# Moving a 64-token tile from the dense expert path to the gathered one, in a one-core decoder-layer kernel

## The chip, the cores and the metric

The kernel runs on one core of a Trainium2 chip. The metric is the device time of one execution in microseconds; lower is better.

## The reference

One layer of a decoder trunk is computed for two groups of tokens with the same weights: a prompt of 1024 tokens and 8 samples of 8 tokens. The layer is RMSNorm, a combined input projection whose columns feed two mixers side by side (retention with 8 heads and RWKV-7 with 8 heads), an output projection, a residual, then a product-key expert mixer (PEER), a residual, a gated per-layer embedding and a last norm. The part around the change is PEER:

```python
q = (xb @ wq).reshape(PEER_BLOCK, PEER_HEADS, 2, PEER_DKEY // 2)
s = jnp.einsum('phcd,hcnd->phcn', q, keys).astype(jnp.float32)
sv, si = lax.top_k(s, PEER_TOPK)
cand = sv[:, :, 0, :, None] + sv[:, :, 1, None, :]
cv, ci = lax.top_k(cand.reshape(PEER_BLOCK, PEER_HEADS, PEER_TOPK * PEER_TOPK), PEER_TOPK)
...
gsm = jax.nn.softmax(cv, axis=-1)
hval = jnp.einsum('pd,phkd->phk', xb, u_tab[e])
act = (jax.nn.gelu(hval.astype(jnp.float32), approximate=False) * gsm).astype(xb.dtype)
return jnp.einsum('phk,phkd->pd', act, v_tab[e])
```

Each token chooses 16 experts in each of 8 heads, 128 of 16384, and each expert is a row of 1024 floats in `u_tab` and one in `v_tab`.

## The kernel before

The tokens are cut into nine tiles: tiles 0 to 7 are the prompt, 128 tokens each, and tile 8 holds the 64 sample tokens (`SIZE`, line 199). PEER is done in two ways.

*Gathered* (tiles 0 and 1, `E0`, and tiles 2 and 3, `G1`): `gather` (line 1115) fetches, for each of the 128 chosen experts, one row of `u_tab` for each of 128 tokens by an indirect DMA on GpSimd (line 1124), multiplies it with the token's row and sums on VectorE (line 1137), applies the gelu and the gate, then fetches the rows of `v_tab` and adds them up in an accumulator in PSUM (line 1151). A fetched tile is 128 x 1024 floats. The result goes to `yd` in memory.

*Dense* (tiles 8, 4, 5, 6, 7, `G2`, 576 tokens): all 16384 experts are computed for all tokens of the group. `hidden` (line 1246) makes the products with `u_tab` for 128 experts at a time, 128 times, each as three matmuls of split operands for 8 blocks of the model width (`mm3`, lines 328 to 330), and a gelu. `gates` (line 1221) builds from the chosen experts a dense gate matrix with one-hot tiles (lines 1235 to 1241) and stores it in `wd`. `act` (line 1262) multiplies the two and splits, and `dense` (line 1275) multiplies with `u`'s partner `v_tab` and adds up in `yT` (lines 1294 and 1301). Columns are cut by `chunks_of` (line 208) into equal parts of at most 512: 576 becomes 288 and 288, so that every weight tile is used in two matmuls.

The order of the work is this. `group_a` makes the input projections; `group_b` (line 650) runs the mixers of the tiles in the order of `BORDER`, as generators that are stepped in turn, with the output projection `c_rows` of finished tiles and, one step at a time, the generator `early` (line 1206). `early` makes the query and the top-k of tile 0 by `early_query` (line 1168), starts tile 0's gather, makes tile 1's query in between as soon as tile 1's rows are there, and then gathers tile 1. At most `EB` = 150 steps of it are taken in `group_b`; what is left is recorded at line 1483, after the query of the dense group (`c_query`, line 1008, in three parts: tiles 2 and 3; 8, 4 and 5; 6 and 7). Then a loop (line 1500) goes over the dense tiles: top-k of one beside the gates of the one before, then a share of the first 96 `hidden` products, stored in `gd`; the gathers of tiles 2 and 3 are recorded in its second and fifth turn (`TK1`). After it `dense_fused` (line 1304) makes the last 32 hidden products beside the first part of the output product, `dense_stored` (line 1323) reads the 96 stored ones back, and `ple` (line 1368) ends the layer tile by tile.

The order in which each engine finally takes its instructions is set by a list scheduler, which takes the recorded order as priority. Row buffers of the early gather are the four tags of `rows` (line 1208), and a fifth for the second tile. PSUM has eight banks: six in `psum` with two for the early accumulator (`psume`), later two for the accumulator `psumg` and six for the rest; in the dense stage `py` has two buffers of two banks.

## Time and profile before

| | |
|---|---|
| runs, us | 3994.43, 4011.38, 4012.78 (median 4011.38) |
| profiled execution, us | 3997.31 |
| its span, us | 3995.5 |
| instructions | 65022 |
| memory read and written, MB | 926.92 and 113.25 |
| mean over the span, GB/s | 260 |

The engine lines of the profile give busy time and its share of the span; the slices are fortieths of the span, some 100 us each. PE is TensorE's matmul, PEld its weight load, DVE VectorE, ACT ScalarE, POOL GpSimd and SP SyncE. In a row of groups the time after the bar is the sum of busy time and the mean of one instruction in ns; after the second bar stands the idle time just before them, with what ended it. Matmuls overlap in the pipeline, so their mean duration is longer than the distance from one to the next. In a row of a window the first number is its length and then comes the busy time of each engine with its count of instructions.

### The profile page before, as it was taken

The numbers are of one execution on the slowest core, as the hardware profiler recorded it, in microseconds if no ns is written. First come the engines' busy times: TensorE is split into PE (matmuls) and PEld (weight loads), VectorE is DVE, ScalarE is ACT, GpSimd is POOL, SyncE is SP. The second block draws the span as 40 slices with busy tenths as digits, with TensorE's granted clock in tenths as the row PEclk, the third lists the DMA queues.
The fourth block names the chain that finished last, engine by engine and source line by source line (L and its number), as shares of the span: only waits on it lengthen the run. The fifth ranks groups of instructions, "written<-read, shape, count | busy, mean of one in ns | idle before, by whom it ended". The sixth has DMA issues, their size and how long they took to land. (4 is left out here: it accounts for less than half of the span.)

```text
span 3995.5 us, 65022 instructions
## 1 busy us (share of the span) xinstructions
PE 3499.3 (88%) x24160; PEld 3210.9 (80%) x24160; DVE 3015.0 (75%) x5720; ACT 1242.6 (31%) x2374; POOL 2090.5 (52%) x1811
## 2 busy tenths in 40 slices
PE   8789986777867888579989999998999899899998
PEld 7688975545746666469989999998999888899977
DVE  4453588977798788761699999975999999995544
ACT  4232221111111121123354667782222222222222
POOL 5363175544456555451346778756767566561110
PEclk9799995567877787689999999999999999999999
DMA  7267467899868898994336889899998999995522
GB/s 259 73 198 239 158 225 256 265 309 285 302 222 295 304 320 285 349 320 146 130 123 220 321 304 352 307 348 333 326 320 316 345 339 360 336 369 183 164 80 70
DMA packets 458774, 1044.47 MB, mean 261 GB/s; under 512 B 71643, under 2 KB 194777, under 8 KB 451930
## 3 DMA queue, kind: packets, MB, share of 16 engines
q0 software_dynamic: 147456, 536.94, 37.9%
q1 hardware_dynamic: 248878, 390.11, 29.6%
q10 hardware_dynamic: 62124, 113.27, 7.5%
q8 instruction: 191, 3.13, 0.3%
q14 instruction: 125, 1.02, 0.1%
HBM read 926.92 MB, written 113.25 MB: 260 GB/s over the span
## 5 line engine op out<-in xcount | busy, mean ns | idle before, releaser
L1124 POOL DMA_INDIRECT grow<-in_pv,eid x512 | 526.3, 1028 | 506.7 <-DVE gacc L1151 386.8
L1151 DVE SCALAR_TENSOR_TENSOR gacc<-grow,ac,gacc 128x1024 f32<-128x1024 f32 x508 | 651.7, 1283 | 95.8 <-DMA grow<-in_pv,eid 90.6
L1124 POOL DMA_INDIRECT grow<-in_pu,eid x512 | 520.8, 1017 | 373.9 <-DVE grow L1137 246.1
L1137 DVE SCALAR_TENSOR_TENSOR grow<-grow,gacc 128x1024 f32<-128x1024 f32 x512 | 613.6, 1211 | 65.6 <-DMA grow<-in_pu,eid 64.6
L328 PE MATMUL ph<-cx,uh 128*128 128x288 f32 x2048 | 615.6, 301 | 29.3 <-ACT geh L1259 29.3
L330 PE MATMUL ph<-cx,ul 128*128 128x288 f32 x2048 | 615.2, 300 | 0.0
L329 PE MATMUL ph<-cx,uh 128*128 128x288 f32 x2048 | 615.1, 300 | 0.0
L1294 PE MATMUL py<-ah,vh 128*128 128x288 f32 x2048 | 442.3, 299 | 27.0 <-DVE yT L1301 15.6
L1294 PE MATMUL py<-ah,vl 128*128 128x288 f32 x2048 | 443.5, 299 | 23.3 <-POOL vl L303 13.5
L1294 PE MATMUL py<-al,vh 128*128 128x288 f32 x2048 | 443.5, 299 | 5.0 <-DVE al L301 4.8
L328 PEld LDWEIGHTS ph<-cx,uh 128*128 128x128 f32 x2048 | 389.3, 190 | 31.5 <-ACT geh L1259 31.5
L329 PEld LDWEIGHTS ph<-cx,uh 128*128 128x128 f32 x2048 | 389.5, 190 | 0.0
L330 PEld LDWEIGHTS ph<-cx,ul 128*128 128x128 f32 x2048 | 389.4, 190 | 0.0
L303 POOL TENSOR_TENSOR ul<-uraw,uh 128x1024 fp32r<-128x1024 f32 x128 | 307.1, 2400 | 150.7 <-ACT uh L299 132.4
L1294 PEld LDWEIGHTS py<-ah,vh 128*128 128x128 f32 x2048 | 330.1, 190 | 35.9 <-ACT vh L299 18.6
L1294 PEld LDWEIGHTS py<-ah,vl 128*128 128x128 f32 x2048 | 331.9, 191 | 29.6 <-POOL vl L303 15.9
L1294 PEld LDWEIGHTS py<-al,vh 128*128 128x128 f32 x2048 | 332.2, 191 | 7.2 <-DVE al L301 7.2
L303 POOL TENSOR_TENSOR vl<-vraw,vh 128x640 fp32r<-128x640 f32 (+2 forms) x112 | 166.9, 1490 | 224.6 <-ACT vh L299 223.5
L299 ACT ACTIVATE vh<-vraw 128x640 fp32r<-128x640 f32 (+2 forms) x224 | 151.9, 688 | 332.9 <-PE py L1294 292.0
L1301 DVE TENSOR_TENSOR yT<-yT,py 128x576 f32<-128x576 f32 x216 | 161.0, 747 | 95.6 <-PE py L1294 95.1
L1237 ACT ACTIVATE oh<-oh,it 128x128 f32<-128x128 f32 x576 | 182.4, 393 | 75.9 <-DVE oh L1235 74.9
L1235 DVE TENSOR_TENSOR oh<-csta,pit 128x512 f32<-128x512 f32 x288 | 184.0, 678 | 24.5 <-PE pwt L1240 24.3
(402 smaller groups left out, 7950.6 us busy)
## 6 DMA issues: line engine op xcount, KB each, us to landing
uraw<-in_puT SPq DMA_DIRECT2D x128, 512.0 KB, 4.4
vraw<-in_pvd SPq DMA_DIRECT2D x152, 320.0 KB, 4.9
wd<-wst ACTq DMA_DIRECT2D x36, 1024.0 KB, 14.2
wt<-wd SPq DMA_DIRECT2D x64, 576.0 KB, 7.1
cw<-in_w_out SPq DMA_DIRECT2D x128, 256.0 KB, 5.5
gd<-geh ACTq DMA_DIRECT2D x96, 288.0 KB, 5.0
ge<-gd SPq DMA_DIRECT2D x96, 288.0 KB, 5.5
wraw<-in_w_ret SPq DMA_DIRECT2D x48, 512.0 KB, 4.9
```

What stands on the lines that cost most here:

```text
L299: nc.scalar.activation(hi, src, AF.Copy)
L303: nc.gpsimd.tensor_tensor(lo, src, hi.bitcast(F32), op=OP.subtract)
L328: mm(out, lh(k), rh(k), start=first and k == 0, stop=False)
L329: mm(out, lh(k), rl(k), start=False, stop=False)
L330: mm(out, ll(k), rh(k), start=False, stop=last and k == nk - 1)
L1124: nc.gpsimd.indirect_dma_start(out=g[:n], out_offset=None, in_=src, in_offset=bass.IndirectOffsetOnAxis(ap=self.eid[t][:n, j:j + 1], axis=0))
L1137: nc.vector.scalar_tensor_tensor(g[:, c], g[:, c], 1.0, x[:, c], op0=OP.mult, op1=OP.mult, accum_out=hv[:, i, j:j + 1])
L1151: nc.vector.scalar_tensor_tensor(y[:, c], g[:, c], ac[:, j:j + 1], y[:, c], op0=OP.mult, op1=OP.add)
L1235: nc.vector.tensor_tensor(oh[j], io, p[:, j, s + b:s + b + 4, None].to_broadcast([128, 4, 128]), op=OP.is_equal)
L1237: nc.scalar.activation(oh[0][:, j], oh[0][:, j], AF.Copy, scale=it[:, s + b + j:s + b + j + 1])
L1294: nc.tensor.matmul(p[:, c, :cn], lh[:, b, :], rh[:, c0:c0 + cn], start=b == 0 and j == 0, stop=b == nb - 1 and j == 2)
L1301: nc.vector.tensor_tensor(yv, yv, pv, op=OP.add)
```

## The change

Tile 8 joins the gathered tiles: `E0` becomes `[0, 1, 8]` and `G2` `[4, 5, 6, 7]`, so that the dense group has 512 tokens, one chunk. A fetch of the gather has 128 rows, and tile 8 has 64 tokens; its 128 experts are therefore laid in two halves, the first 64 on partitions 0 to 63 and the others on 64 to 127, and 64 fetches of each table serve it. Its input row is loaded twice, its two partial sums go to `yd` as 128 rows, and `ple` adds both. Its query is the single-tile `early_query`, now for 64 rows, recorded behind tile 1's query with tile 0's gather in between, and ahead of the gathers of tiles 1 and 8. All gathers use one accumulator pool of two banks, opened at the start. `c_query` has two parts instead of three, the loop over the dense tiles one turn fewer, and `py` has four buffers of one bank.

```diff
-E0 = [0, 1]
+E0 = [0, 1, 8]
-G2 = [8, 4, 5, 6, 7]
+G2 = [4, 5, 6, 7]
...
-                    for _ in range(ERATE if self.rowed >= set(E0) else 0):
+                    for _ in range(ERATE if E0[1] in self.rowed else 0):
...
+        elif t == 8:
+            gsm = tp.tile([128, 128], F32, name="gsm8", tag="cf")
...
+        if t == 8:
+            ei = tp.tile([128, 128], I32, name="ei", tag="ex")
+            nc.vector.tensor_copy(ei[:n], ef[:n])
+            for k in range(2):
+                nc.scalar.dma_start(self.eid[t][64 * k:64 * k + 64], ei[:64, 64 * k:64 * k + 64])
+                nc.scalar.dma_start(self.gsm[t][64 * k:64 * k + 64], gsm[:64, 64 * k:64 * k + 64])
...
     def gather(self, gp, t, rows=("grow",), parts=1, acc=None):
-        n = 128
+        n = SIZE[t]
...
-        nc.sync.dma_start(x, self.xd[t])
+        for k in range(0, 128, n):
+            nc.sync.dma_start(x[k:k + n], self.xd[t][:n])
...
     def early(self, wp):
-        g = self.behind(self.gather(wp, E0[0], rows, acc=self.acc0), PG0)
-        while not self.rowed >= set(E0):
-            next(g, None)
-            yield
-        q = self.behind(self.early_query(wp, E0[1], "Wq", 1, ("Wq", "xT")), PQ1)
-        for _ in q:
-            next(g, None)
-            yield
+        g = self.gather(wp, E0[0], rows, acc=self.acc)
+        for t in E0[1:]:
+            while t not in self.rowed:
+                next(g, None)
+                yield
+            for _ in self.early_query(wp, t, "Wq", 1, ("Wq", "xT")):
+                next(g, None)
+                yield
         yield from g
-        yield from self.gather(wp, E0[1], rows + ("xT",), acc=self.acc0)
+        for t in E0[1:]:
+            yield from self.gather(wp, t, rows + ("xT",), acc=self.acc)
...
-                p = self.ps2.tile([128, 2, 512], F32, name="py")
+                p = self.ps2.tile([128, ncx, 512], F32, name="py")
...
-                y = tp.tile([128, D], F32, name="py", tag="njunk")
-                nc.sync.dma_start(y, self.yd[t])
-                nc.vector.tensor_tensor(h, h, y, op=OP.add)
+                for k in range(0, 128, n):
+                    y = tp.tile([128, D], F32, name="py", tag="njunk")
+                    nc.sync.dma_start(y[:n], self.yd[t][k:k + n])
+                    nc.vector.tensor_tensor(h[:n], h[:n], y[:n], op=OP.add)
...
+            acc = self.acc = self.pool("psumg", space=PS, es=eg, reuse_waits="tile")
             self.psums("psum", ep, a=2, b=3, d=1)
-            self.acc0 = self.pool("psume", space=PS, es=ep, reuse_waits="tile")
...
-            parts = [G1, G2[:QA], G2[QA:]]
+            parts = [G1, G2]
...
-            acc = self.pool("psumg", space=PS, es=eg, reuse_waits="tile")
...
-                    self.ps2 = self.pool("psumy", bufs=2, space=PS, es=e2, reuse_waits="tile")
+                    self.ps2 = self.pool("psumy", bufs=4 // len(self.chunks), space=PS, es=e2, reuse_waits="tile")
```

`early_query` takes `n = SIZE[t]` rows in place of 128 throughout.

More of the change, by code (lines that the diff above doesn't have):

```diff
@@ L181 @@
 CN = 2
-QA = 3
 BORDER = [1, 8, 2, 3, 4, 5, 6, 7]
@@ L187 @@
 IB = 2
-PG0 = 0
-PQ1 = 0
 PGT = "a"
@@ L1029, in c_query @@
                     nc.tensor.matmul(p[:SIZE[t], i * 128:i * 128 + 128], qT[:, off[t]:off[t] + SIZE[t]], kT, start=True, stop=True)
-                i0 = tiles.count(8)
-                if i0:
-                    nc.scalar.activation(s[:64, 0, hc % 2], p[:64, :128], AF.Copy)
-                nc.scalar.activation(s[:, i0:, hc % 2], p[:, i0 * 128:len(tiles) * 128].rearrange("p (t k) -> p t k", k=128), AF.Copy)
+                nc.scalar.activation(s[:, :, hc % 2], p[:, :len(tiles) * 128].rearrange("p (t k) -> p t k", k=128), AF.Copy)
                 if hc % 2:
@@ L1123, in fetch @@
             g = slot("grow", rows[j % len(rows)])
-            nc.gpsimd.indirect_dma_start(out=g[:n], out_offset=None, in_=src,
-                                         in_offset=bass.IndirectOffsetOnAxis(ap=self.eid[t][:n, j:j + 1], axis=0))
+            nc.gpsimd.indirect_dma_start(out=g, out_offset=None, in_=src,
+                                         in_offset=bass.IndirectOffsetOnAxis(ap=self.eid[t][:, j:j + 1], axis=0))
             return g
         x = slot("gx", rows[-1])
-        nc.sync.dma_start(x, self.xd[t])
+        for k in range(0, 128, n):
+            nc.sync.dma_start(x[k:k + n], self.xd[t][:n])
         xs, x = x, home()
         nc.scalar.activation(x, xs, AF.Copy)
-        hv = gp.tile([128, parts, 128], F32, name="hv")
+        hv = gp.tile([128, parts, 128], F32, name="hv")[:, :, :n]
         cs = [slice(i * D // parts, (i + 1) * D // parts) for i in range(parts)]
@@ L1138, in gather @@
             yield j
-        ac = gp.tile([128, 128], F32, name="ac")
+        ac = gp.tile([128, 128], F32, name="ac")[:, :n]
         for i in range(1, parts):
@@ L1189, in early_query @@
             for k in range(8):
[L1190 removed]
+                nc.tensor.matmul(p[:, :n], w[:, k], xT[:, k, :n], start=k == 0, stop=k == 7)
             qT = wp.tile([128, 128], F32, name="eqT", tag=("cf", "ef")[hc % 2])
[L1192 to L1194 removed]
+            nc.scalar.activation(qT[:, :n], p[:, :n], AF.Copy)
+            nc.tensor.matmul(p[:n, 128:256], qT[:, :n], kT, start=True, stop=True)
+            nc.scalar.activation(st[:n, hc % 2], p[:n, 128:256], AF.Copy)
             if hc % 2:
[L1196 removed]
+                nc.scalar.dma_start(self.sd[t][:n, hc - 1:hc + 1], st[:n])
             yield
@@ L1467, in build @@
             self.e12 = {}
-            n2, n3 = spans(G2[:QA])[1], spans(G2[:-1])[1]
-            query = self.c_query(cq, da, [(G1, x1), (G2[:QA], [y[:, :, :n2] for y in x]), (G2[QA:], [y[:, :, n2:] for y in x])])
+            n3 = spans(G2[:-1])[1]
+            query = self.c_query(cq, da, [(G1, x1), (G2, x)])
             def rest():
```

22 lines of the change are left out of this document (9 added, 13 removed).

## Prediction

> **What bounds the kernel now.** I read the page first: its engine totals and the 40 slices.
>
> ```profile
> span 3995.5 us, 65022 instructions
> PE 3499.3 (88%) x24160; PEld 3210.9 (80%) x24160; DVE 3015.0 (75%) x5720; ACT 1242.6 (31%) x2374; POOL 2090.5 (52%) x1811
> DVE  4453588977798788761699999975999999995544
> PEclk9799995567877787689999999999999999999999
> DMA  7267467899868898994336889899998999995522
> ```
>
> No engine binds everywhere, so I cut the span at landmarks of the program (first gather, the third tile's keys, first `wql`, first `oh`, first `yT`, the 64th, last gather, first `ppg`) and asked for busy time by stage. Columns: us, busy us of PE, PEld, DVE, ACT, POOL, granted clock, DMA share, GB/s.
>
> ```profile
> 1083.00:1725.00 642.00, 488.37 (x2648) 372.72 (x2647) 534.74 (x1013) 106.33 (x205) 352.83 (x350) 0.76 0.84 295
> 1725.00:2046.00 321.00, 299.09 (x2193) 288.44 (x2191) 183.34 (x736) 96.78 (x193) 124.95 (x94) 0.96 0.52 182
> 2046.00:2754.00 708.00, 666.26 (x5116) 661.08 (x5117) 627.29 (x1516) 466.06 (x989) 482.47 (x356) 0.98 0.81 296
> 2754.00:3163.00 409.00, 397.14 (x2958) 394.34 (x2957) 374.50 (x432) 110.90 (x188) 280.02 (x226) 0.99 0.92 326
> 3163.00:3600.00 437.00, 401.15 (x2860) 389.83 (x2860) 401.37 (x450) 117.30 (x173) 271.93 (x221) 0.97 0.98 349
> 3600.00:3835.00 235.00, 229.55 (x1716) 226.46 (x1714) 118.38 (x159) 63.32 (x94) 46.31 (x31) 1.00 0.50 156
> ```
>
> Mixers (to 1725): nothing saturated, a chain of waits with gathers in its gaps. Query and top-k (to 2046): PE 93%. Gates beside hidden products (to 2754): PE 94%, DVE 89%. Fused dense (to 3163): PE 97%, DMA 0.92. Stored dense with gathers (to 3600): DMA 0.98. Then 235 us of dense product alone, DMA at 0.50: room that no gather uses. Dense steps (`yT` additions) in these last three: 64, 95, 65.
>
> **The change, part by part.** *Price of the dense matmuls.* The chain has a run of 288-column ones, the order-of-time view 512-column ones in `ple` (first and last of 21 in a row):
>
> ```profile
> 3747.67 80.09 PE py L1294 x604
> ...
> 3928.08 0.39 PE L328 MATMUL ppg<-pga,pxh 128*128 128x512 f32 x1
> ...
> 3932.75 0.39 PE L330 MATMUL ppg<-pgx,pxl 128*128 128x512 f32 x1
> ```
>
> 80.09/604 = 0.1326 us each, and 4.67/20 = 0.2335. A pair of 288 (0.2652) becomes one of 512: 0.0317 us less. Hidden and output products are 3072 pairs each, so 6144 x 0.0317 = 195 us of PE time goes, and 16 x 24 x 0.0317 = 12 in the query, where 320 + 256 columns become 512.
>
> *Price of the gathers.* Tile 8 adds 64 + 64 fetches.
>
> ```profile
> L1124 POOL DMA_INDIRECT grow<-in_pv,eid x512 | 526.3, 1028 | 506.7 <-DVE gacc L1151 386.8
> L1151 DVE SCALAR_TENSOR_TENSOR gacc<-grow,ac,gacc 128x1024 f32<-128x1024 f32 x508 | 651.7, 1283 | 95.8 <-DMA grow<-in_pv,eid 90.6
> L1137 DVE SCALAR_TENSOR_TENSOR grow<-grow,gacc 128x1024 f32<-128x1024 f32 x512 | 613.6, 1211 | 65.6 <-DMA grow<-in_pu,eid 64.6
> L1137 DVE DVE_READ_ACCUMULATOR grow<-grow,gacc 128x1 f32 x512 | 40.8, 80 | 0.0
> q0 software_dynamic: 147456, 536.94, 37.9%
> ```
>
> One costs DVE (1283 + 1211 + 80)/2 = 1.287 us, POOL 1.03 us and the DMA 536.94/1024 = 0.524 MB. So +165 us DVE, +132 us POOL, +67 MB. Against that tile 8 leaves the gates, a ninth of the `oh`, `wst` and `wd` work below, and its top-k moves from the stage after the query into the mixers.
>
> ```profile
> L1235 DVE TENSOR_TENSOR oh<-csta,pit 128x512 f32<-128x512 f32 x288 | 184.0, 678 | 24.5 <-PE pwt L1240 24.3
> L1237 ACT ACTIVATE oh<-oh,it 128x128 f32<-128x128 f32 x576 | 182.4, 393 | 75.9 <-DVE oh L1235 74.9
> L303 POOL TENSOR_TENSOR ul<-uraw,uh 128x1024 fp32r<-128x1024 f32 x128 | 307.1, 2400 | 150.7 <-ACT uh L299 132.4
> L1241 ACT ACTIVATE wst<-pwt 128x512 f32<-128x512 f32 x144 | 157.6, 1106 | 43.6 <-PE pwt L1240 34.3 <-PE ph L330 4.6 <-issue 2.7
> L1050 DVE FIND_INDEX8 si<-sv,s 128x8 uint32<-128x128 f32 x96 | 25.9, 278 | 0.0
> L1088 DVE TENSOR_TENSOR eq<-csta,cf 128x800 f32<-128x800 f32 x64 | 80.1, 1251 | 0.3
> L1090 DVE TENSOR_REDUCE ef<-eq 128x16 f32<-128x800 f32 x64 | 62.4, 975 | 12.4 <-POOL eq L1089 12.3
> uraw<-in_puT SPq DMA_DIRECT2D x128, 512.0 KB, 4.4
> vraw<-in_pvd SPq DMA_DIRECT2D x152, 320.0 KB, 4.9
> wd<-wst ACTq DMA_DIRECT2D x36, 1024.0 KB, 14.2
> wt<-wd SPq DMA_DIRECT2D x64, 576.0 KB, 7.1
> gd<-geh ACTq DMA_DIRECT2D x96, 288.0 KB, 5.0
> ```
>
> A top-k costs DVE five passes like L1050 on 16 rows (80 x 0.27 = 22 us), eight `eq` and `ef` (8 x 142.5/64 = 18) and 40 short ones that I put at 5: 45 us, of 64 rows as of 128, since the row's length is the same. The `oh` of tile 8 are 32 x 0.678 = 22 us.
>
> *Where they go.* The lists of instructions of the two built programs give the order. When the query starts, 464 gather steps stand ahead on DVE before and 396 after; at the first `yT`, 703 and 804; at the 64th, 863 and 939; the last stands after the 159th of 224 `yT` before, after the 197th now. Before, PE has 17 of the 96 early hidden products ahead of the first gate matmul; after, 84. So the gates become a stage of their own, with DVE, ACT and DMA in it and little for PE.
>
> *Mixers.* The query of tile 8 stands between the third tile's and the fifth's chain, and tile 1's gather waits behind it in the program: two mixers with 19 and no gathers, then about as many as before; 68 fewer by the start of the query. Mixers and the fetches alone in them (us, POOL busy us and count, clock, DMA share, GB/s), and the matmuls of tile 1's query in the first of them:
>
> ```profile
> 957.00:1152.00 195.00, 66.34 (x67) 0.81 0.83 273
> 1152.00:1256.00 104.00, 36.59 (x35) 0.81 0.80 271
> 1256.00:1366.00 110.00, 47.98 (x49) 0.79 0.89 315
> L1190 PE MATMUL epq<-exT,ewq 128*128 128x128 f32 x191 | 32.8, 332 | 5.6 <-DMA ewq<-in_wq 4.7 <-ACT ktk L819 0.7
> ```
>
> 14 more fetches went with 6 us: 0.43 each, so 68 fewer are worth 29 us; were the mixers bound by fetches (110/49 = 2.2 each), 150. The new query has 256 such matmuls of half the width: at 32.8/191 each at most 44 us of PE, and if it stretches a mixer as tile 1's may have done (195 against 104), 91. I take 19 of the 44, since PE is idle a quarter of this stage: -29 + 19 = **-10** (ends -150 and +91; the mixers of 104 and 110 are the nearest rows). Its 16 weight loads of 512 KB go out on SP into one buffer, and its top-k on DVE, in a time without gathers: 45 us come, 68 x 1.287 = 88 go. Before 1083 the order is the same.
>
> *Query, top-k and hidden* (to the first `oh`). PE had 299 busy us, 17 hidden products (17 x 48 x 0.1326 = 108) in them; now 299 - 108 - 12 + 84 x 24 x 0.2335 = 650. DVE, in this stage and the gates together: 183 + 627 = 811 before, now 408 gather steps for 239 (+217), a top-k and its `oh` fewer (-67): 961, of which 385 fall to the gates (below) and 576 here. Fetches are 244 x 0.524 = 128 MB here, the rest as before. PE is the longest; at 96%: 677 us.
>
> *Gates.* 256 `oh` x 0.678 + 164 gathers x 1.287 = 385 us of DVE; ACT (182.4 + 157.6) x 8/9 = 302; PE 12 hidden products, 67 us, and the gate matmuls; DMA 164 x 0.524 = 86 MB of fetches, 32 x 1.05 = 34 of `wd`, some 16 of hidden and first dense loads. Rows for what such a mix reaches (all engines, then the fetches alone, then all engines again):
>
> ```profile
> 2300.00:2500.00 200.00, 192.20 (x1487) 191.33 (x1486) 193.13 (x487) 139.63 (x291) 155.78 (x118) 0.98 0.89 328
> 2500.00:2700.00 200.00, 63.55 (x66) 1.00 0.89 329
> 3300.00:3400.00 100.00, 91.57 (x643) 88.86 (x642) 95.91 (x98) 28.02 (x41) 65.10 (x54) 0.95 1.01 363
> ```
>
> 136 MB at 328 GB/s is 415 us, DVE's 385 at 92% are 418: I take 425. Both stages: 677 + 425 = 1102 against 321 + 708 = 1029, **+73**: PE's saving here is lost, since its work no longer lies beside the gates.
>
> *Fused dense.* 28 hidden products and 64 steps of 12: (672 + 768) x 0.2335 = 336 us of PE, at 97% 346; 135 gathers for 160, so DVE 375 - 25 x 1.287 and some 20 for narrower tiles = 323. Both would be over 90% busy: I take 352, against 409.
>
> *Stored dense, to the last gather.* 133 steps with 213 gathers, for 95 with 160. PE 133 x 15 x 0.2335 = 466. DVE: 401 - 160 x 1.287 = 195 for 95 steps, so 133 x 1.87 (eight ninths of most) + 213 x 1.287 = 523, at the 92% of before 570. DMA 112 MB of fetches, 44 of `vraw`, 44 of `ge` and `wt`, 5 of gate weights: 205 at 349 GB/s = 587. I take 577, against 437. The tail: 27 steps, the last eight of one block, 309 x 0.2335 = 72, against 235. Dense together 1001 against 1081: **-80**. PSUM: four one-bank `py` stand for two of two banks; PE waited 15.6 us for these at most, inside stages that DMA and DVE now set, so 0:
>
> ```profile
> L1294 PE MATMUL py<-ah,vh 128*128 128x288 f32 x2048 | 442.3, 299 | 27.0 <-DVE yT L1301 15.6
> ```
>
> The 205 MB are priced by the saturated rows (share 0.98 at 349 GB/s, 1.01 at 363). The Trainium skill, DMA: Bandwidth & Descriptors, "Where 436 GB/s comes from", puts the port ceiling at 435 GB/s and one core's share of the memory, both cores streaming, at about 358. By the first the estimate would be 471 us, DVE would bind at 570 and the sum would be 7 us less; the rows agree with the second, though one core runs here.
>
> *`ple`.* Tile 8 reads two halves of `yd` instead of eight transposes, in a stretch that PE fills: 0 (+-3). One accumulator pair for all tiles: gathers follow each other through it already; 0.
>
> Sum on the profiled run: 3997.3 - 10 + 73 - 80 = **3980**. Its runs had a median of 4011, 14 above it; 0.5% (20 us) is about what a measurement tells from no change.
>
> **Rivals.** (1) *The freed room is used.* For it: DMA stood at 0.52 from 1725 to 2046. If both stages before dense go at DVE's 961 us, 95% busy, they take 1012, -17, and if the query hides, the mixers give -29: 3997 - 29 - 17 - 80 = **3871**. Against it: PE alone wants 650 before the gates start, and DVE was 89% busy in the gates. (2) *The gate stage stalls.* From 2500 to 2700, with gates, 66 fetches took 200 us, 3.03 each; 164 at that price are 497 instead of 425: **4052**, slower. It decides from about 462 us for the stage. Against it: hidden loads shared the DMA there. (3) *The clock falls.* Stored dense leaves PE 80% busy, and mixers ran at 0.76 with PE 76% busy. At 0.76, 466 becomes 613: +36, **4016**; at half speed 932, far outside. Against it: 0.97 at 92%. The Trainium skill, TensorE: Matmul & The Clock Gate, "HAM oscillation", says that idle gaps over about 3.4 us drop the array to half clock. The longest wait of PE between 3130 and 3600 is 2.9 us (us in all, times, longest), so by that rule the clock stays:
>
> ```profile
> PEld py L1294 <- POOL vl L303: 12.5, 7, 2.9
> ```
>
> (4) *It doesn't do what it says*: the lists show that it does, no chance given.
>
> **How the numbers follow.** Forecast 3980, own range 3945 to 4015: 0.42, 0.19 of it faster by 0.5%, 0.02 slower (a mixer stretched by the query). Room used: 0.26. Gate stage stalls: 0.24. Clock: 0.08, half within 0.5%. Faster 0.19 + 0.26 = 0.45; slower 0.02 + 0.24 + 0.04 = 0.30; same 0.21 + 0.04 = 0.25. Range 3860 to 4075: from the first rival, with a little of the fetches' larger price, to the second with a quarter of the query's larger one.
>
> **What would show it.** `py` at 0.23 us a matmul, a tail near 72 us, first `oh` some 680 us after the first `wql` and the first `yT` some 425 later, PE well under 70% busy between. Wrong would be: mixers of 80 us where no gathers stand (then faster), gathers at over 3 us in the gates, or a clock under 0.9 in stored dense (slower).

## The result, and the profile after

The changed kernel takes 4112.38 us (median of 4 runs, 4101.5 to 4121.27) against 4011.59 for the kernel before in the same session: a ratio of 1.026, 95% interval 1.022 to 1.030. It is slower by about 100 us, and outside the range of the prediction. One of the four executions of the third experiment below took 9462.73 us, in a slow state, and is left out of its median. The page of the changed kernel, engine totals and slices:

```profile
span 4117.0 us, 52401 instructions
PE 3449.2 (84%) x17749; PEld 2831.4 (69%) x17749; DVE 3165.3 (77%) x5876; ACT 1172.9 (28%) x2149; POOL 2212.5 (54%) x1939
DVE  4453579877881588776799988898799989999844
PEclk9799986577775678769999999866799999999999
DMA  7267478899772368899988888888899999999822
```

Two holes are new. In slices 13 and 14 (1235 to 1441 us) VectorE falls to 0.1 and 0.5, DMA to 0.2 and 0.3 and the clock to 0.5 and 0.6. In slices 26 to 29 the clock is at 0.6 to 0.8; that is the stage of the gates. The same landmarks as in the prediction cut the span: `wql` is the low half of the dense query's split weights, `oh` a one-hot tile of the gates, `yT` the accumulated output (us, then busy us of PE, PEld, DVE, ACT and POOL with counts, clock, DMA share, GB/s):

```profile
1083.00:1821.00 738.00, 582.53 (x2976) 460.33 (x2975) 508.29 (x1172) 115.83 (x240) 303.79 (x300) 0.71 0.65 225
1821.00:2518.00 697.00, 632.84 (x2950) 521.85 (x2949) 598.13 (x1633) 196.61 (x268) 529.08 (x399) 0.96 0.88 307
2518.00:2968.00 450.00, 309.72 (x1484) 269.62 (x1483) 391.94 (x598) 308.00 (x691) 236.86 (x210) 0.75 0.86 311
2968.00:3320.00 352.00, 341.10 (x1458) 274.63 (x1456) 337.22 (x359) 98.45 (x155) 249.38 (x200) 0.99 0.93 332
3320.00:3880.00 560.00, 492.14 (x1955) 368.64 (x1954) 517.87 (x645) 151.12 (x231) 350.56 (x287) 0.97 0.98 352
3880.00:3950.00 70.00, 69.12 (x298) 54.89 (x298) 38.37 (x58) 20.62 (x34) 16.22 (x13) 1.00 0.47 144
3950.00:4117.00 167.00, 140.71 (x638) 110.60 (x638) 80.97 (x119) 43.74 (x81) 13.40 (x36) 0.93 0.24 77
```

| stage | before | after | difference | forecast |
|---|---|---|---|---|
| mixers, to the first `wql` | 642 | 738 | +96 | -10 |
| query, top-k, hidden, gates, to the first `yT` | 1046 | 1147 | +101 | +73 |
| dense product, to the last `yT` | 1064 | 982 | -82 | -80 |
| `ple` | 160 | 167 | +7 | 0 |

Before is cut at 2771 here, where the first `yT` stands; the prediction's 2754 is the first `py` matmul, 17 us earlier. The differences add up to 122, which is 4117.0 - 3995.5 rounded. The last two rows came out near what was forecast, and the second 28 above it. Most of the loss that the prediction had not priced, 106 us, lies in the mixers. The fetches alone, in the same three mixers that the prediction showed (POOL busy us and count, clock, DMA share, GB/s):

```profile
957.00:1156.00 199.00, 63.98 (x65) 0.76 0.81 265
1156.00:1276.00 120.00, 20.18 (x19) 0.76 0.60 198
1276.00:1468.00 192.00, 0.00 (x0) 0.60 0.27 87
```

The first mixer is 4 us longer than before. The second is 16 us longer and the third 82, with no fetch in it and TensorE at a clock of 0.60.

### The profile page after: what moved, and what is told of

Read it like the earlier page. It is cut to its first block, busy times and chain, and to the rows that moved or that the text cites. A ratio compares the mean times of both kernels' runs of the same rounds, so it can differ in the third digit from the quotient of the medians.

```text
span 4117.0 us, 52401 instructions
## 1 busy us (share of the span) xinstructions
PE 3449.2 (84%) x17749; PEld 2831.4 (69%) x17749; DVE 3165.3 (77%) x5876; ACT 1172.9 (28%) x2149; POOL 2212.5 (54%) x1939
## 5 line engine op out<-in xcount | busy, mean ns | idle before, releaser
L1300 PE MATMUL py<-ah,vl 128*128 128x512 f32 x1024 | 412.1, 408 | 49.4 <-DVE vl L298 32.0
L1300 PE MATMUL py<-ah,vh 128*128 128x512 f32 x1024 | 413.0, 407 | 38.4 <-ACT ah L296 25.2
L325 PE MATMUL ph<-cx,uh 128*128 128x512 f32 x1024 | 409.8, 400 | 23.2 <-ACT geh L1265 14.7
L327 PE MATMUL ph<-cx,ul 128*128 128x512 f32 x1024 | 406.6, 399 | 19.5 <-POOL ul L300 19.5
L1300 PE MATMUL py<-al,vh 128*128 128x512 f32 x1024 | 411.5, 402 | 3.1 <-DVE al L298 3.1
L326 PE MATMUL ph<-cx,uh 128*128 128x512 f32 x1024 | 406.4, 397 | 0.0
L1246 PE MATMUL pwt<-oh,oh 128*128 128x128 f32 x1024 | 202.5, 365 | 122.8 <-ACT oh L1243 105.1
L1246 PEld LDWEIGHTS pwt<-oh,oh 128*128 128x128 f32 x1024 | 182.9, 260 | 143.9 <-ACT oh L1243 141.8
L325 PEld LDWEIGHTS ph<-cx,uh 128*128 128x128 f32 x1024 | 196.7, 192 | 68.7 <-ACT geh L1265 17.4
L327 PEld LDWEIGHTS ph<-cx,ul 128*128 128x128 f32 x1024 | 196.6, 192 | 67.7 <-POOL ul L300 26.4
L296 ACT ACTIVATE uh<-uraw 128x1024 fp32r<-128x1024 f32 x128 | 135.5, 1059 | 360.3 <-DMA uraw<-in_puT 276.9
L326 PEld LDWEIGHTS ph<-cx,uh 128*128 128x128 f32 x1024 | 197.1, 192 | 41.2
```

The lines of the kernel that those rows point to most:

```text
L296: nc.scalar.activation(hi, src, AF.Copy)
L325: mm(out, lh(k), rh(k), start=first and k == 0, stop=False)
L326: mm(out, lh(k), rl(k), start=False, stop=False)
L327: mm(out, ll(k), rh(k), start=False, stop=last and k == nk - 1)
L1246: nc.tensor.matmul(pw[:, j, :], oh[1][:, j, :], oh[0][:, j, :], start=True, stop=True)
L1300: nc.tensor.matmul(p[:, c, :cn], lh[:, b, :], rh[:, c0:c0 + cn], start=b == 0 and j == 0, stop=b == nb - 1 and j == 2)
```

## The experiments

Theory A: the half tile's query, 16 projections in series, with the mixer's own instructions behind them in the built order of each engine, stretches two mixers. Its rivals: the gathers do it (B), the single weight buffer does it (A1), the low clock does it (A2, later C). The kernel before had medians of 3998.6 to 4008.8 us beside these runs; 4112 below is the changed kernel, measured beside 4011.6. So times of different sessions can differ by some 13 us; the ratios leave that out. This is one table for all fourteen, with the stages cut as above and, where gathers outlast the dense product, by how much.

| run | us | ratio to before, interval | mixers | query to first one-hot | gates | dense |
|---|---|---|---|---|---|---|
| changed kernel | 4112.4 | 1.026, 1.022 to 1.030 | 738 | 697 | 450 | 982 |
| 1 no query of the half tile | 3914.8 | 0.977, 0.975 to 0.980 | 648 | 517 | 524 | 980 |
| 2 two weight buffers | 4189.8 | 1.045, 1.042 to 1.049 | 619 | 901 | 428 | 990 |
| 3 gather beside the query | 4104.7 | 1.025, 1.022 to 1.027 | 635 | 794 | 448 | 985 |
| 4 query with the dense ones | 3979.5 | 0.993, 0.991 to 0.996 | 651 | 326 | 670 | 991, then 213 |
| 5 half tile left out | 3817.9 | 0.952, 0.949 to 0.955 | 639 | 310 | 626 | 1002 |
| 6 gate buffers apart, one `wst` | 4061.8 | 1.014, 1.011 to 1.018 | 723 | 371 | 705 | 1001, then 53 |
| 7 one `wst` | 4180.3 | 1.043, 1.040 to 1.046 | 732 | 699 | 529 | 969 |
| 8 query in a first pass | 3985.6 | 0.994, 0.992 to 0.996 | 603 | 632 | 513 | 986 |
| 9 gate buffers apart | 3971.2 | 0.994, 0.991 to 0.996 | 707 | 327 | 679 | 994, then 137 |
| 10 = 4 and 9 | 3981.7 | 0.996, 0.993 to 0.999 | 653 | 317 | 715 | 991, then 176 |
| 11 = 8 and 9 | 3939.3 | 0.984, 0.981 to 0.988 | 610 | 420 | 665 | 999, then 1 |
| 12 query of 128 columns | 4056.3 | 1.013, 1.009 to 1.016 | 681 | 695 | 450 | 984 |
| 13 64 columns, twice | 4153.2 | 1.034, 1.030 to 1.038 | 769 | 695 | 449 | 993 |
| 14 = 9 and 12 | 3947.0 | 0.985, 0.982 to 0.988 | 691 | 324 | 694 | 989, then 123 |

### 1: no query of the half tile

```diff
+            if t == 8:
+                self.nc.vector.tensor_copy(self.eid[8], self.eid[1][:, :64])
+                self.nc.vector.tensor_copy(self.gsm[8], self.gsm[1][:, :64])
+                continue
             for _ in self.early_query(wp, t, "Wq", 1, ("Wq", "xT")):
```

> Leaves out the query and the top-k of the half tile: its list of experts and its weights are copied from the first 64 columns of tile 1's, so the same number of rows is gathered, of other experts. Theory A (the serial chain of the half tile's query, 16 projections some 9 us apart with the mixer's own instructions queued behind them on the in-order engines, stretches the mixers of 1156 to 1468): the two mixers come back to about 105 us each, the first dense query weights are loaded some 95 us earlier (about 1725 where it was 1821), and the time falls from 4112 to about 4015. Rival B (the mixers are long because more rows are gathered beside them, on VectorE and in the DMA queues, and the query is only what happens to stand there): the gathers move up into the place of the query, the mixers stay within 20 us of 738 in sum, and the time falls by less than 25, to about 4090. If the later stages are late for reasons of their own (gates and hidden products, +45 beyond what was forecast), 4015 is still above the time before without the dense gain, and the stage between the first one-hot and the fused products stays near 450.

The mixers came back to 648, as theory A had it and B had not. But the time fell by 198, not by 95. The fetches by stage, first of the changed kernel, then of this one, show the rest:

```profile
1083.00:1821.00 738.00, 178.74 (x180) 0.71 0.65 225
1821.00:2518.00 697.00, 237.69 (x235) 0.96 0.88 307
```

```profile
1083.00:1731.00 648.00, 248.66 (x250) 0.76 0.84 293
1731.00:2248.00 517.00, 161.60 (x165) 0.95 0.86 299
```

Ahead of the first one-hot both kernels make the same fetches (with 226 and 227 before 1083, 641 and 642). Here 70 more of them fit into mixers that are 90 us shorter. In the changed kernel those 70 stand in the next stage and make it 180 us longer; 74 of it come back at the gates, because hidden products move ahead of them (2950 TensorE instructions for 2265 in the one stage, 1484 for 2190 at the gates). So the query costs twice: 90 in the mixers, and 106 by the gather steps that it displaced. The removal of the top-k is in these numbers too.

### 2: two weight buffers

```diff
-            for _ in self.early_query(wp, t, "Wq", 1, ("Wq", "xT")):
+            for _ in self.early_query(wp, t, *(("V", 2) if t == 8 else ("Wq", 1)), ("Wq", "xT")):
```

> The half tile's query weights in two buffers where there was one; everything else as in the changed kernel. Theory A1 (each projection waits for a load that can only be issued once the projection before it has left the single buffer, some 5 us of the 9 us of each): the projections come every 5 us or so, the two stretched mixers lose about 50 to 60 us together, the time falls to about 4060. Rival A2 (the projection is slow because TensorE runs at a granted clock of 0.5 with narrow 64-column products, and the chain through ScalarE sets the pace): the projections stay about 9 us apart and the time stays within 15 us of 4112. Rival B (the gathers stretch the mixers): no change either.

Both were wrong: 77 us slower than the changed kernel. The two buffers are two of the gather's rows, so tile 0's gather stood still while the query ran: 126 fetches before 1083 instead of 226. The query ended earlier, the mixers were 119 us shorter (619), and the missing steps appeared in the next stage:

```profile
0.00:1083.00 1083.00, 127.33 (x126) 0.84 0.61 193
1702.00:2603.00 901.00, 324.24 (x328) 0.91 0.88 306
```

Together with the first run this gives a price: 165 steps in 517 us, 235 in 697, 328 in 901. From the first to the last, (901 - 517)/163 = 2.4 us for each step that stands between the first `wql` and the first one-hot. The loads of the query into TensorE (count, ns least, median and most, first and last start) are these:

```profile
L1195 PEld LDWEIGHTS epq<-exT,ewq x256: 186/333/338, 1127.0 to 1238.9; 128*128 128x128 f32 x128
```

The projections came every 111.9/16 = 7.0 us, where the changed kernel has 9.0 (run 12 below), so between the two expectations. How much of that is the second buffer is not shown, since other work stood beside them; TensorE waited little for the query weights in either kernel, 0.7 us here and 5.5 in the changed one. A buffer of its own for the query, beside the gather's rows, was not tried.

### 3: tile 1's gather beside the query

```diff
+            yield from g
+            g = self.gather(wp, t, rows + (("xT",) if t == E0[-1] else ()), acc=self.acc)
         yield from g
-        for t in E0[1:]:
-            yield from self.gather(wp, t, rows + ("xT",), acc=self.acc)
```

> Tile 1's gather is recorded beside the half tile's query, where the changed kernel leaves the queue of gathers empty from 1276 to 1468 (no or few rows fetched). Theory A (the query's chain holds the mixers): the mixers stay as long or grow by up to 40 us more, since each step of the query now also stands behind row products on VectorE; but about 60 rows more are gathered before the dense query, and the rest of the early gather ends earlier, which is worth up to 60 us in the stage of the gates if the gathers set its end, and nothing if the half-clocked gates set it. Time between 4060 and 4150. Rival G (the gap of the gathers is the loss itself): about 4040.

4104.7: no difference to the changed kernel. The built order put the query behind the mixers (its last projection began at 2024, not at 1382). Mixers of 635, and the next stage 97 us longer with 44 steps fewer in it (us, busy us of five engines, clock, DMA share, GB/s):

```profile
1718.00:2512.00 794.00, 673.26 (x3078) 553.24 (x3079) 603.03 (x1820) 192.36 (x287) 496.76 (x376) 0.89 0.71 246
```

By the price of the second run 191 steps would take 517 + 26 x 2.4 = 579 of the 794. By this estimate the query costs 215 us there, about as much as the 196 in the changed kernel. That the place makes no difference is argued from that price and not tested by itself. The row of the query alone and its weight loads:

```profile
1907.00:2027.00 120.00, 71.13 (x292) 61.56 (x293) 112.17 (x700) 9.73 (x35) 21.28 (x24) 0.50 0.36 116
L1195 PEld LDWEIGHTS epq<-exT,ewq x256: 285/333/338, 1907.5 to 2024.1; 128*128 128x128 f32 x128
```

With hardly any other work for TensorE its projections still take 116.6/16 = 7.3 us each, and in 16 waits TensorE lost 49.0 us to the loads into the one buffer, 3.1 each. Here the single buffer is a good part of the period.

### 4: the query with the dense ones

```diff
-E0 = [0, 1, 8]
-G1 = [2, 3]
+E0 = [0, 1]
+G1 = [8, 2, 3]
-TK1 = {2: 1, 3: 4}
+TK1 = {8: 0, 2: 1, 3: 4}
...
+                i0 = tiles.count(8)
+                if i0:
+                    nc.scalar.activation(s[:64, 0, hc % 2], p[:64, :128], AF.Copy)
...
```

> The half tile leaves the early queries: its query is made with the dense ones (320 and 512 columns instead of 256 and 512), its top-k comes first in the gate loop, and its 64 columns of fetched rows pairs follow there. The dense products stay at 512 tokens. Theory A: the mixers come back to about 640 (95 us less), the dense query's first part grows from 256 to 320 columns (as before the change: about 16 us), the gathers of the half tile come late, beside the gates, where they may stretch the stage by some 64 x 2 rows of some 1 us of VectorE that nothing hid before (0 to 60 us). Sum: 4112 - 95 + 16 + (0 to 60): 4033 to 4095, most likely 4050. Rival B (the gathers make the mixers long): mixers 20 us shorter at most, and the time at 4110 or above.

3979.5, 133 us under the changed kernel and 29 under the kernel before. The mixers are at 651 again. The query takes 326 us with 320 columns and 512. The half tile's gather now comes late, and the gathers end 213 us after the last `yT`. The estimate of 4050 was too high; it had taken the displaced steps for free in the changed kernel and charged them here.

### 5: the half tile left out

```diff
-        for t in E0[1:]:
+        for t in E0[1:2]:
...
-                for k in range(0, 128, n):
+                for k in range(0, 128 if t != 8 else 0, n):
```

> Leaves out the half tile's expert mixer altogether: no query, no top-k, no gather of it, and nothing added for it at the end. The dense products stay at 512 tokens, so this is what the narrower dense group is worth with nothing put in its place, and with the first experiment it prices the 128 fetches: 3915 there, which had them without their query. Theory S (a gather step that stands ahead of the first one-hot lengthens that stage by what it costs there, 180 us for 70 steps between the first experiment and the changed kernel, 2.5 each): 128 steps are worth up to 320 us, the time is 3600 to 3650. Theory T (the stages go by the sums of TensorE and VectorE work, as the forecast had it: 129 us less in query and gates, 166 less in dense than before the change): about 3700, that is 1.7 us a step. Rival F (the fetches hide beside other work): 3850 or more.

3817.9: theory S's 3600 to 3650 and T's 3700 are both wrong, and F's 3850 is the nearest. Against the first run 128 gather steps are worth 97 us, 0.76 each, less than VectorE's own 1.29. The price of 2.4 above holds only where the steps decide when the next stage may start. Stage by stage it misses T's numbers in the dense product:

```profile
2032.00:2658.00 626.00, 577.67 (x2979) 487.48 (x2979) 522.13 (x1230) 412.36 (x821) 418.61 (x299) 0.98 0.80 289
2658.00:3641.00 983.00, 896.02 (x3632) 692.88 (x3631) 910.68 (x1058) 269.55 (x412) 630.24 (x511) 0.96 0.95 336
```

T had 915 for the dense product; with 359 fetches of tiles 2 and 3 beside it, DMA at 0.95 and VectorE at 93%, it takes 1002. All the kernels with 512 tokens have 969 to 1002 there. The change now splits into three, by medians of the runs: 512 tokens for 576 without the half tile, 3817.9 - 4006.9 = -189; its gather, +97; its query with its top-k, +198. The sum is +106, for 101 in the changed kernel's own session.

### 6 and 7: what lies between the gathers and the gates

In the built order the first one-hot stands on VectorE behind all 640 early gather steps, in the changed kernel and in the first three runs. VectorE's order of time in the changed kernel shows it (start, us; the last step of the early gather and the first one-hot):

```profile
2513.95 1.29 DVE L1155 SCALAR_TENSOR_TENSOR gacc<-grow,ac,gacc 128x1024 f32<-128x1024 f32 x1 [2.96 <-DMA grow<-in_pv,eid]
...
2517.80 2.46 DVE L1241 TENSOR_TENSOR oh<-csta,pit 128x512 f32<-128x512 f32 x4
```

Nothing in the data asks for that; the gates' buffers lie in the memory that the early gather's rows leave. The kernel before had it too: 227 + 246 + 40 = 513 fetches stand ahead of its first one-hot, and its early gather has 512 steps. There only 40 of them fell behind the first `wql`. The sixth kernel keeps the early pool open over the gate loop and opens the gather's own pool on the other side. Room for it was made with one `wst` buffer, and the seventh has that alone.

```diff
             ew.close()
-            ee.close()
             ep.close()
...
-            gp = sb("gat", eg, side="right")
...
+            gp = sb("gat", eg)
             tp = sb("tk", et)
...
             et.close()
+            ee.close()
...
-            st = wp.tile([128, 128, 64], F32, name="wst", bufs=2)
+            st = wp.tile([128, 128, 64], F32, name="wst", bufs=1)
```

> The gates' one-hot and store buffers no longer lie where the early gather's rows lay (the early pool is closed after the gate loop, the gather's own pool opened ahead of it on the other side; to make room the store tile wst has one buffer for two). The built order then has the first one-hot behind 530 gather steps on VectorE where the changed kernel has it behind all 640. Theory M (the memory shared by the early rows and the one-hots makes two stages of what could be one): the first one-hot starts some 300 us earlier, and the 1147 us from the first wql to the first yT become about 1050 (VectorE's 990 busy us at 94%), so the time falls to about 4015. Rival N (DMA at 0.87 and VectorE at 0.87 in both stages already set their sum, the order within them does not matter): 1147 stays within 25, and the time is 4090 to 4140.

> The control of the run before: the changed kernel with one buffer for wst instead of two, nothing else. If the store of a block hides behind the next block's one-hots only with two buffers, each of the 8 blocks waits some 10 us more: up to 80 us, 4190; if something else sets the pace of the gates, 0 to 15 us: 4112 to 4127, which I take for likelier.

The control lost 68 us, where I had taken 0 to 15: 79 more at the gates (529 for 450), of which 13 came back in the dense product. Against that control the sixth gains 118: its first one-hot starts at 2177 instead of 2514, and first `wql` to first `yT` takes 1076 instead of 1228. Theory N is out. The direct expectation, 4015, failed by 47 us; the price of the one buffer, 68 in the control, is enough for that.

### 8: the query in a first pass

Built on the fourth kernel, with the half tile's gather last among the early ones.

```diff
-            query = self.c_query(cq, da, [(G1, x1), (G2, x)])
+            query = self.c_query(cq, da, [(G2, x)])
...
             run(self.rows_in(cn, G1, x1))
+            run(self.c_query(cq, da, [(G1, x1)]))
+            run(self.topk(tp, 8))
             run(rest())
...
             run(query)
             run(early)
+            run(self.gather(ep0, 8, ("V", "V", "W", "xy", "xT"), acc=acc))
```

> A better place for the half tile: its query is made with tiles 2 and 3 (320 columns) in a pass of its own ahead of the pass for the 512 dense tokens, its top-k follows at once, and its gather is the last of the early ones, beside the dense query, where DMA stood at 0.53 and VectorE at 176 of 326 us in the fourth experiment. No serial single-tile query in the mixers, no gather left behind the dense product (213 us of the fourth experiment). Theory A with S: mixers 650, then as in the first experiment (3915), 16 us for the wider query and some 25 us for reading the query weights twice: about 3955. Rival (the top-k comes too late or its work on VectorE holds the weight splits, so that the room of the query stays unused): 4000 to 4050.

3985.6, between the two expectations. The tail of gathers is gone, but now 640 steps stand ahead of the first one-hot again, and the stage before it takes 632 where the fourth's took 326. Same time, other place.

### 9 to 11: the gate buffers apart, with both store buffers

```diff
-            gp = sb("gat", eg, side="right")
...
-                            run(self.behind(self.gather(gp, t, acc=acc), PG))
+                            run(self.behind(self.gather(ep0, t, ("V", "V", "W", "xy", "xT"), acc=acc), PG))
...
-            ee.close()
...
             eg.close()
+            ee.close()
...
-        ex = tp.tile([128, 8, 16], F32, name="ex")
+        ex = tp.tile([128, 8, 16], F32, name="ex", tag="ci")
...
-            pt = tp.tile([128, 2, 128], F32, name="pt", bufs=2)
+            pt = tp.tile([128, 2, 128], F32, name="pt", bufs=1)
```

> The sixth experiment without its side effect: the gates' buffers lie apart from the early gather's rows, and the store tile keeps its two buffers. For room the gathers of tiles 2 and 3 use the early gather's five rows instead of a pool of their own (five rows as well), two scratch tags of the top-k are shared, and the last stage's small tile pt has one buffer. First one-hot behind 523 gather steps in the built order, 51 steps left after the last dense step. Theory M: what the sixth gained over its control, 118 us of 4180, is gained here from 4112: 3994, plus up to 30 for the gather that outlasts the dense product. Rival: the gain was only the repair of the single store buffer's own loss (which then hid behind gathers), so that it stays at 4090 to 4112.

> The same memory layout on the fourth experiment's kernel (half tile's query with the dense ones, top-k in the gate loop). There the first one-hot stood behind 512 gather steps, all there were, at 2060, some 330 us after the first wql, so nothing was held by the shared memory. Theory M: no gain at the gates, 3965 to 3985 (3980 before). If it gains over 40 us, M is not the (whole) mechanism of the ninth.

> The same memory layout on the eighth experiment's kernel (query of tiles 8, 2, 3 in a first pass, gather of the half tile beside the dense query), where all 640 early steps stand ahead of the first one-hot; now 594. Theories A and M together: no serial query in the mixers, and gates that overlap with the gathers: 3986 less some 90: about 3890, below the time before the change (4007 in these runs) and below the fourth's 3980. Rival (what is freed at the gates comes back in the stored dense stage, where DMA is at 0.96): 3950 to 3990.

The ninth is the changed kernel with nothing but this: 3971.2, 141 us less (129 by the ratios to the kernel before, 0.994 for 1.026), and just under the kernel before. Its stages from the first `wql` to the first `yT`:

```profile
1790.00:2117.00 327.00, 299.46 (x1565) 254.90 (x1564) 238.23 (x457) 91.89 (x137) 223.82 (x178) 0.96 0.91 325
2117.00:2796.00 679.00, 582.83 (x2868) 490.21 (x2868) 637.75 (x1667) 417.61 (x819) 474.81 (x363) 0.90 0.88 312
```

1006 us instead of 1147: TensorE now has 583 busy us beside the gates where it had 310. (The mixers, at 707, are 31 shorter as well, with another order of the built program; the dense product and `ple` give 25 back.) The tenth is the test of the reason. The fourth kernel has no gather step left to hold its first one-hot, and the same layout gains nothing there (3981.7 for 3979.5; 45 us more at the gates and 37 less behind the dense product). The eleventh gains 46 on the eighth, half of what I expected; its 3939.3 is the lowest time of the kernels that do the whole work, 1.6% below the kernel before. Its stages:

```profile
1083.00:1693.00 610.00, 468.65 (x2562) 364.14 (x2562) 522.99 (x989) 101.59 (x197) 345.93 (x344) 0.76 0.85 295
1693.00:2113.00 420.00, 354.01 (x1638) 287.26 (x1639) 304.58 (x723) 115.95 (x180) 264.08 (x206) 0.90 0.83 296
2778.00:3778.00 1000.00, 912.09 (x3700) 696.43 (x3698) 934.43 (x1090) 267.88 (x416) 644.37 (x530) 0.97 0.96 339
```

No gather is left behind the dense product, and that product, with DMA at 0.96, is as long as in every other run.

### 12 and 13: why the query is slow

```diff
-        n = SIZE[t]
+        n = 128
         xn = wp.tile([128, D], F32, name="exn", tag=wtag, bufs=wbufs)
-        nc.sync.dma_start(xn[:n], self.xd[t][:n])
+        for k in range(0, 128, SIZE[t]):
+            nc.sync.dma_start(xn[k:k + SIZE[t]], self.xd[t][:SIZE[t]])
```

> The half tile's early query with 128 columns (its 64 rows twice), as wide as tile 1's; nothing else. Theory A (16 loads into one buffer, each behind the projection before it, set the pace of some 9 us): the mixers of 1156 to 1468 stay within 15 us of 312 and the time within 15 us of 4112. Rival C (the granted clock of 0.5 in them comes from products that are too narrow, and wider ones lift it): those mixers some 40 us shorter, 4070. Rival W (TensorE's own time counts): 256 products of 0.33 instead of about 0.2 us, up to 30 us more, 4140.

Twice the columns made the kernel 56 us faster. The projections of the changed kernel and then of this one (count, duration ns least, median and most, first and last start), with their weight loads under them:

```profile
L1195 PE MATMUL epq<-exT,ewq x256: 274/421/475, 1237.3 to 1382.0; 128*128 128x64 f32 x128
L1195 PEld LDWEIGHTS epq<-exT,ewq x256: 185/333/338, 1237.3 to 1381.9; 128*128 128x128 f32 x128
```

```profile
L1196 PE MATMUL epq<-exT,ewq x256: 274/276/580, 1235.4 to 1336.0; 128*128 128x128 f32 x128
L1196 PEld LDWEIGHTS epq<-exT,ewq x256: 186/192/338, 1235.4 to 1335.9; 128*128 128x128 f32 x128
```

The same 256 loads of the same shape take 333 ns in the median instead of 192, beside a clock of 0.50 and 0.92 in the rows below; more columns did not make the query slower. One of the 16 projections comes every 144.7/16 = 9.0 us in the one, every 100.6/16 = 6.3 in the other. The whole query, changed kernel first:

```profile
1237.00:1386.00 149.00, 142.14 (x664) 127.14 (x662) 24.84 (x51) 19.01 (x51) 11.17 (x8) 0.55 0.24 75
1235.00:1338.00 103.00, 92.87 (x643) 85.09 (x641) 23.26 (x51) 18.76 (x50) 10.28 (x8) 0.87 0.36 108
```

TensorE is busy for 142 of the 149 us, 56 of them in the query's own projections (41 of 103 in the twelfth); the rest is the mixers' work at the same low clock. So it is not a chain of waits that fills this stretch but TensorE, and theory A's pace by the single buffer is out here. The stretch from 1276 on, again changed kernel first:

```profile
1276.00:1340.00 64.00, 58.40 (x242) 50.49 (x243) 6.18 (x11) 8.76 (x24) 6.48 (x5) 0.50 0.28 83
1340.00:1400.00 60.00, 56.51 (x301) 52.43 (x300) 18.82 (x84) 9.71 (x22) 0.00 (x0) 0.59 0.24 78
```

```profile
1276.00:1340.00 64.00, 56.73 (x447) 53.34 (x447) 10.74 (x25) 15.36 (x39) 0.00 (x0) 0.92 0.41 127
```

447 matmuls in the 64 us for 242, at 0.92 for 0.50, with TensorE busy 57 and 58 of the 64 us. The thirteenth asks whether it is the amount of work:

```diff
-            for k in range(8):
+            for k in [k for _ in range(128 // n) for k in range(8)]:
                 nc.tensor.matmul(p[:, :n], w[:, k], xT[:, k, :n], start=k == 0, stop=k == 7)
```

> The half tile's query stays 64 columns wide, but each group of eight projections is issued twice into the same bank (the second overwrites the first): as many column steps as in the twelfth experiment, 256 narrow matmuls instead of 128 wide ones, 128 more weight loads in TensorE. In the changed kernel the granted clock was 0.50 from 1276 to 1340, in the twelfth 0.92, and the whole query took 149 us there against 103. Theory R (the share of streaming to weight loading sets the granted clock, so a narrow product keeps it low however many there are): clock at 0.5 to 0.6, the query 15 to 30 us longer, time 4125 to 4150. Theory D (any more work of TensorE per load of 512 KB lifts the clock): clock over 0.8 and the query near 105 us, time 4060 to 4080.

It is not. Twice as many narrow products left the clock where it was, and the query took 195 us, 46 more than in the changed kernel, where I had taken 15 to 30:

```profile
L1195 PE MATMUL epq<-exT,ewq x512: 275/421/476, 1230.6 to 1423.2; 128*128 128x64 f32 x171
```

```profile
1276.00:1340.00 64.00, 55.89 (x228) 48.39 (x229) 4.51 (x6) 5.06 (x15) 3.58 (x2) 0.50 0.22 64
1340.00:1400.00 60.00, 60.00 (x281) 57.99 (x280) 4.24 (x10) 6.38 (x16) 0.00 (x0) 0.50 0.17 50
```

From 1340 to 1400 TensorE was busy 60.00 of 60 us and stayed at 0.50. Theory R holds in these runs: a chain of 64-column products, each beside its weight load, keeps the clock low, however many there are. The second and third run, with the query in other places, agree: their loads have a median of 333 ns too. The Trainium skill, TensorE: Matmul & The Clock Gate, "What's actually happening", has the clock rise after some 3.4 us of sustained activity; by that rule the thirteenth run's second row would stand near 1. It shows 60 us of activity without a rise, and here the measurement decides. The Trainium skill, TensorE: Matmul & The Clock Gate, "Why this matters for your kernels", says that thin products are to be regrouped or padded. The twelfth run padded them, from 64 to 128 columns, and the clock went to 0.92.

### 14: both causes together

The ninth and the twelfth kernel's edits in one.

> The ninth and the twelfth experiment together: gates' buffers apart from the early gather's rows, and the half tile's query 128 columns wide. If the two causes are apart from each other, the gains add: 4112 - 141 - 56 = 3915, faster than the kernel before the change (4000) and than the eleventh (3939). If the earlier end of the mixers only lengthens the tail of gathers behind the dense product (137 us in the ninth), 3950 to 3970.

3947.0: 24 below the ninth (35 by the ratios), not 56, and just under the range for the second case. The first `wql` came 16 us earlier, where the twelfth had 57, and the gathers still outlast the dense product by 123 us. The two gains do not add. Why they don't is not shown; that both bring forward the same gathers is my guess.

## Why the prediction was wrong, point by point

- **Mixers, -10: the step that failed.** Measured +96, so 106 of the 139 us between the forecast of -17 and the 122 of the two profiles. The step priced the new query by TensorE's busy time, at most 44 us at the clock of the 128-column query, and took 19 of that on the ground that TensorE idles a quarter of the stage. The runs show in its place: beside the 64-column products the clock went to 0.50, the projections alone were busy 56 us and not 44, the query lasted 149 us with TensorE busy for 142, and no row was fetched from 1276 to 1468. Without the query the mixers are 90 us shorter (first run); with 128 columns they are 57 shorter (738 to 681, twelfth run). What makes the other 33 is not separated. The end of +91, read from the mixers of 195 and 104, was listed and kept for the tail with a chance of 0.02; it is close to what was measured.
- **The 68 fewer fetches in the mixers, -29.** The number was right, 66 (180 for 246). Whether fewer fetches shorten the mixers no run shows by itself. What the prediction lacked is their price in the next stage: it let them hide there beside TensorE's 650, but 70 displaced steps cost 180 us before the first one-hot, of which 74 came back at the gates, 106 net (first run).
- **Query and hidden products, 677:** 697 measured, with 235 fetches for 244 and TensorE busy for 633 where 650 was forecast. The numbers held, the reason did not, and that is luck: TensorE was not what ended the stage. The ninth, where the same stage takes 327, shows that the end of the early gather did, since the gates wait for its memory.
- **Gates, 425:** 450, and TensorE 310 of 450, 69%, not well under the 70% that was named. The clock fell to 0.75 in this stage; what that costs no run tests.
- **Rival 1, the freed room is used, 1012 for both stages:** this was near the figure for a kernel without the shared memory (1006 in the ninth), though by luck: it had VectorE at 961 us, 95% busy, and the ninth has 876, 87%, with 47 fetches left behind the dense product. The prediction held the built order against it, 84 hidden products ahead of the first gate, and did not ask what made that order.
- **Dense product:** 352 for 352, 560 for 577, 70 for 72, and the 298 matmuls of the tail in 69.12 us, 0.232 each. Right. The stage takes 969 to 1002 us in all runs, with the half tile or without. In the fifth DMA stands at 0.95, VectorE at 93% and TensorE at 91%; which of them binds was not tested. The price of 349 GB/s held (352 at 0.98 from 3320 to 3880), but the prediction's rows are no ceiling: from 1660 to 1670 the kernel before moved 416 GB/s at a share of 1.02.
- **Rivals 2 and 3:** the gate stage stayed under the 462 from which the second decides, and the clock in stored dense stayed at 0.97. It fell where no rival had it, in the mixers (0.76 to 0.71) and at the gates (0.98 to 0.75).
- **`ple`, 0:** +7, a small miss that was not tested by itself.
- **One accumulator pair:** no run was made on it. With the query of the fourth run the kernel is faster than before with that pair in place; what the pair itself costs was not measured.

What stays open: how much of the remaining 6.3 us a projection in the twelfth would go with a second weight buffer, why the granted clock stays at 0.50 with narrow products, and at what width between 64 and 128 columns it rises.

## What to carry to other kernels

A chain of small dependent steps that is put into an already interleaved stage lasts its period times its count (149 us here). It stretches the stage by a part of that (90), and it costs what it displaces, priced where that work lands (106). Busy time taken at another clock said little (44 us at most), and the nearest row of a like chain (195 against 104) said most. Where a built order shows a stage starting exactly behind the last step of another, ask whether data or only memory puts it there; moving the buffers was worth some 130 to 140 us here. And a product that halves its columns need not be half as long: in these runs the clock halved at 64 columns instead.

## What was not expected of the hardware

With 64-column fp32 products the granted clock was 0.50 through 60 us in which TensorE was busy all the time; from 1276 to 1340, where 64 columns had 0.50, 128 columns gave 0.92, and the median weight load went from 333 to 192 ns.
